# Two small SBUF tiles made larger in a two-layer hybrid decoder trunk

## The chip, the cores and the metric

The kernel runs on one NeuronCore of one Trainium2 chip, in one launch. The metric is the device time of one execution in microseconds (us); several executions are timed and their median is given. One further execution is recorded by the hardware profiler: its span runs from the first to the last instruction.

The engines are TensorE (PE; its weight loads are shown as PEld), VectorE (DVE), ScalarE (ACT), GpSimd (POOL) and SyncE (SP, which here only issues DMAs).

## The reference

The kernel computes a trunk of two layers over 256 positions of width 1,024, in float32. Each layer normalises its input, projects it through one matrix of 1,024 x 3,584, runs three branches, gates them, and projects back with a residual:

```python
def hybrid_layer(x, ...):
    hn = rms_norm(x, norm_gain)
    proj = jnp.einsum('bsd,de->bse', hn, w_in)
    a_q, a_k, a_v, a_g, b_x, b_g, c_q, c_k, c_v, c_g = jnp.split(proj, ...)
    y_a = dilated_attention(rope(a_q), rope(a_k), a_v) * silu(a_g)    # 8 heads of 64
    y_b = rg_lru_branch(b_x, conv_w, ...) * silu(b_g)                 # width 256
    y_c = stick_breaking_attention(c_q, c_k, c_v) * silu(c_g)         # 4 heads of 64
    y = jnp.concatenate([y_a, y_b, y_c], axis=-1)
    return x + jnp.einsum('bse,ed->bsd', y, w_out)
```

A last normalisation follows the second layer. The branch b begins with a causal convolution of width 4 along the sequence.

## The kernel before

**Arithmetic.** Each large product is made from three float32r products. A tile is split into a high part (rounded to float32r by ACT) and a low part (what is left, by DVE), and hi x hi, hi x lo and lo x hi are added in PSUM. The normalised input is the tile `xx`, which holds `xh` and `xl` side by side. Weights come from HBM in chunks of 128 x 2,048 through staging tiles `st` and are split into `whi` (line 109) and `wlo` (line 110). The gated branch outputs are split into `yh` and `yl` (lines 413 and 414), the rotated q and k into tiles that the profile calls `qk` (lines 498 and 499).

**Matmul lines.** Line 169 is the first projection, made while the first chunks arrive. Line 211 is the helper `mm3`, used by several projections: those whose moving tile is xx (256 columns, stationary tile whi or wlo; named `pp<-xx,whi`), those of a_v and c_v in layer 1 (stationary xx, moving whi or wlo), and the output projection (stationary yh or yl, moving whi or wlo, 512 columns). In the names of the profile the two operands of a matmul stand in no fixed order. Lines 330 and 327 make the paired projections of layer 1: line 330 takes xh and xl together as 512 moving columns, line 327 takes 256. Line 513 makes the scores of the dilated attention, four heads at a time on 32 rows each. Line 461 holds transposes.

**Order of the work.** PE's instructions run in the order in which the program writes them. SP issues the weight loads in the order of use, limited by free staging tiles. ACT and DVE split the weights ahead of PE into four buffers each for whi and wlo.

**Where tiles lie.** SBUF tiles come from the pools cst, wst, wsp, sb and wk, laid one behind the other in this order in each partition; inside a pool they lie in the order in which their tags first appear, with sizes rounded up to 32 bytes. So a size of one tile sets where everything behind it starts. The start of each tile in bytes, past a multiple of 512:

| pool | tiles in order | start before |
|---|---|---|
| cst | xres, con, then `tiny` | 256 |
| cst | ones, c8, nc8 | 288, 288, 320 |
| cst | rp, rp0, rb, gn (and gf) | 352 |
| wst, wsp | st (5 buffers), whi and wlo (4 each) | 352 |
| sb | xx, th, it, va, vc, gw_t, qc (q1), kc (k1), then `bxp` (and av) | 352 |
| sb | xc, xs, rt, bg, cg, q0, k0, yh, yl, the qk tiles | 384 |
| wk | scr (7 buffers), sw, wv | 448 |
| wk | pr, low | 64, 192 |

The slices that PE reads within xx, whi, wlo, yh, yl and the qk tiles step by multiples of 512 bytes, so they have their tile's start.

**The two tiles.** `tiny` holds one number per partition, a bias of 1e-19 for a logarithm in `lru_scan`. `bxp` holds the input of the convolution with three zeros ahead of each of its two halves:

```python
def conv(mid):
    dve.memset(bxp[:, :, 0:3], 0.0)
    proj_to(bxp[:, :, 3:259], CH_BX, mid)
    for b in range(2):
        ...
        for j in (2, 1, 0):
            dve.scalar_tensor_tensor(xc[:, b, :], bxp[:, b, j:j + 256], ...)
```

The tile av of `lru_scan` takes the same place as bxp later in the layer.

Of the kernel before, what the change touches and what calls it, by code (L numbers as in the profile page):

```python
# [9 lines left out]
F32 = mybir.dt.float32  # L10
# [5 lines left out]
P = 128  # L16
# [32 lines left out]
def trunk_kernel(ctx: ExitStack, tc: tile.TileContext, x, first_x, first, wpack, prm_d, gatew, gains, consts, rope, out):  # L49
# [3 lines left out]
    cst = ctx.enter_context(tc.tile_pool(name="cst", bufs=1))  # L53
    wst = ctx.enter_context(tc.tile_pool(name="wst", bufs=WST))
    wsp = ctx.enter_context(tc.tile_pool(name="wsp", bufs=4))
    sb = ctx.enter_context(tc.tile_pool(name="sb", bufs=1))
# [125 lines left out]
    diag = con[:, C_DG:C_DG + 255]  # L182
    nc.sync.dma_start(out=con, in_=consts)

    tiny = cst.tile([P, 1], F32, name="tiny")
    dve.memset(tiny, 1e-19)
    ones = cst.tile([P, P], F32, name="ones")
    dve.memset(ones, 1.0)
# [108 lines left out]
    for l in range(L):  # L297
# [245 lines left out]
            turned(prob, h0, range(3), to)  # L543
            return heads

        bxp = sb.tile([P, 2, 259], F32, name="bxp", tag="bxp")
        xc = sb.tile([P, 2, S], F32, name="xc", tag="xc")
        xs = sb.tile([P, 2, S], F32, name="xs", tag="xs")
        rt = sb.tile([P, 2, S], F32, name="rt", tag="rt")
# [248 lines left out]
```

## Time and profile before

| | before |
|---|---|
| median of 3 runs | 249.22 us (248.92 to 249.33) |
| profiled execution, span | 247.5 us |
| outside the span, against the median | 1.7 us |
| PE busy | 239.7 us, 97% |
| PE weight loads busy | 212.8 us, 86% |
| DVE busy | 193.4 us, 78% |
| ACT busy | 170.8 us, 69% |
| POOL busy | 11.6 us, 5% |
| share of PE in the chain that ended last | 85% |
| DMA | 43.90 MB, mean 177 GB/s |

The page gives no time of its own for the profiled execution beside its span, so the span is what sums are made against. A busy share is a mean over the whole span. The chain that ended last is followed back from the last instruction, at each step to what released it. A matmul's duration contains its latency, which overlaps with the next matmul; the pace at which matmuls follow each other is shorter than that duration.

### The profile page before, as it was taken

To read this page: it belongs to the slowest core of one execution; us is meant where nothing else is said; L and a number is where in the kernel's file an instruction comes from. 1 tells how busy PE (TensorE), PEld (TensorE's weight loads), DVE (VectorE), ACT (ScalarE), POOL (GpSimd) and SP (SyncE) were. 2 spreads that over 40 slices of the span, in tenths; PEclk is the share of its full clock that TensorE was granted. 3 is DMA by queue.
4 is the path that set the end of the run, shared out by engine and by line. 5 is a ranking of instruction groups with operands and counts; after the bars stand their busy time and mean duration, and the time that the engine had idled before them with its cause. 6 is when DMAs were issued, how large, how long until landed. Compare 5 with 4: busy or idle time off the path is not lost.

```text
span 247.5 us, 4741 instructions
## 1 busy us (share of the span) xinstructions
PE 239.7 (97%) x1753; PEld 212.8 (86%) x1753; DVE 193.4 (78%) x454; ACT 170.8 (69%) x368; POOL 11.6 (5%) x45
## 2 busy tenths in 40 slices
PE   8999999999999999999999999999999999999990
PEld 4889999998998899878889988888889889987870
DVE  4884798979999789985693666999999867984253
ACT  3779988844688499964662775876589749992142
POOL 0037000000100000000000000000000000000000
PEclk9999999999999999999999999999999999999997
DMA  6989987377737732267258387506461752000022
GB/s 209 399 284 411 355 318 277 117 234 242 222 98 212 256 98 74 89 218 272 103 171 252 106 304 269 173 3 216 145 193 68 238 209 85 3 0 0 3 85 85
DMA packets 13174, 43.90 MB, mean 177 GB/s; under 512 B 1632, under 2 KB 2144, under 8 KB 13152
## 3 DMA queue, kind: packets, MB, share of 16 engines
q1 hardware_dynamic: 12384, 42.30, 50.6%
q10 hardware_dynamic: 576, 0.79, 0.9%
q0 software_dynamic: 192, 0.52, 0.8%
q8 instruction: 14, 0.23, 0.3%
q14 instruction: 8, 0.07, 0.1%
HBM read 42.03 MB, written 1.05 MB: 174 GB/s over the span
## 4 chain that ended last, share of the span: by engine, by line
PE 85%; DVE 5%; DMA 4%; ACT 2%; SPq 0%; issue 0%; ACTq 0%; DVEq 0%
PE pp L211 44%; PE pp L330 11%; PE s L211 9%; PE pp L327 5%; PE s L169 3%; PE s L461 3%; DMA st<-first 3%; PE s L513 2%; PE y L425 2%; DMA st<-w_pack 2%; PE pp L169 2%; DVE sw L452 2%; DVE wlo L110 1%; PE pp L425 1%; PE s L441 1%; PE s L572 1%
## 5 line engine op out<-in xcount | busy, mean ns | idle before, releaser
L110 DVE TENSOR_TENSOR wlo<-st,whi 128x512 fp32r<-128x512 f32 x132 | 84.0, 684 | 12.4 <-ACT whi L109 12.0
L109 ACT ACTIVATE whi<-st 128x512 fp32r<-128x512 f32 x132 | 74.0, 628 | 20.5 <-PE pp L211 7.6
L211 PE MATMUL pp<-xx,whi 128*128 128x256 f32 x480 | 63.3, 285 | 0.0
L211 PEld LDWEIGHTS pp<-xx,whi 128*128 128x128 f32 x480 | 59.6, 192 | 0.8 <-issue 0.3
L211 PE MATMUL pp<-xx,wlo 128*128 128x256 f32 x240 | 33.7, 283 | 0.0
L211 PEld LDWEIGHTS pp<-xx,wlo 128*128 128x128 f32 x240 | 31.0, 192 | 0.0
L330 PE MATMUL pp<-xx,whi 128*128 128x512 f32 x112 | 29.3, 396 | 0.0
L330 PEld LDWEIGHTS pp<-xx,whi 128*128 128x128 f32 x112 | 20.1, 189 | 3.9 <-ACT scr L83 0.3
L83 ACT ACTIVATE pr<-scr,mn 128x128 f32<-128x128 f32 (+1 forms) x32 | 14.1, 441 | 8.7 <-DVE mn L520 8.7
L77 ACT ACT_TABLE_LOAD x13 | 16.7, 1283 | 1.9 <-PEq L791 1.7
L327 PEld LDWEIGHTS pp<-xx,wlo 128*128 128x128 f32 x112 | 15.3, 190 | 1.1
L327 PE MATMUL pp<-xx,wlo 128*128 128x256 f32 x112 | 15.6, 282 | 0.0
L211 PE MATMUL pp<-whi,yh 128*128 128x512 f32 x48 | 14.6, 405 | 0.0
L211 PE MATMUL pp<-whi,yl 128*128 128x512 f32 x48 | 14.1, 396 | 0.0
L211 PE MATMUL pp<-wlo,yh 128*128 128x512 f32 x48 | 14.1, 395 | 0.0
L211 PEld LDWEIGHTS pp<-whi,yl 128*128 128x128 f32 x48 | 9.0, 188 | 2.2
L211 PEld LDWEIGHTS pp<-wlo,yh 128*128 128x128 f32 x48 | 9.0, 188 | 2.2
L211 PEld LDWEIGHTS pp<-whi,yh 128*128 128x128 f32 x48 | 8.6, 188 | 2.1 <-issue 0.3
L413 ACT ACTIVATE yh<-scr 128x512 fp32r<-128x512 f32 x8 | 5.0, 631 | 7.5 <-DVE scr L411 7.4
L169 PE MATMUL s<-whi,xx 128*128 128x512 f32 (+1 forms) x36 | 9.9, 396 | 0.1
L520 DVE CUSTOM_DVE_ANT_0 scr<-s,con 128x128 f32<-128x128 f32 (+1 forms) x32 | 9.2, 352 | 0.0
L333 ACT ACTIVATE low<-pp 128x256 f32<-128x256 f32 x14 | 5.3, 377 | 5.2 <-PE pp L330 5.2
(175 smaller groups left out, 359.3 us busy)
## 6 DMA issues: line engine op xcount, KB each, us to landing
st<-w_pack SPq DMA_DIRECT2D x66, 512.0 KB, 5.1
st<-first SPq DMA_DIRECT2D x7, 512.0 KB, 6.1
xres<-x_in SPq DMA_DIRECT2D x2, 512.0 KB, 7.5
gw_t<-gate_w SPq DMA_DIRECT2D x2, 256.0 KB, 6.8
gn<-gains SPq DMA_DIRECT2D x1, 512.0 KB, 6.9
xs<-xc POOLq DMA_DIRECT2D x4, 128.0 KB, 4.8
gf<-gains SPq DMA_DIRECT2D x1, 512.0 KB, 6.3
out<-scr SPq DMA_DIRECT2D x2, 256.0 KB, 2.1
```

Source lines behind the costliest of these rows:

```text
L77: load = act.preload_act_table_set(name)
L83: i = dep(act.activation(*a, **k), loaded["load"])
L109: split[l, c] = act.activation(hi[:, ws], st[:, ss], AF.Copy)
L110: dve.tensor_sub(lo[:, ws], st[:, ss], hi[:, ws].bitcast(F32))
L169: pe.matmul(ps[t][:, c0 - base:c1 - base], a[:, k, t * P:(t + 1) * P], b[:, c0:c1], start=k == 0 and i == 0 and c0 == base, stop=k == NK - ...
L211: pe.matmul(ps, a(k), b(k), start=first and i == 0, stop=last and i == len(seq) - 1)
L327: pe.matmul(ps[:, 0:S], lo[:, k, cs], xh[:, k, :], start=False, stop=False, skip_group_check=True)
L330: pe.matmul(ps, hi[:, k, cs], xx[:, k].rearrange("p h t -> p (h t)"), start=i == 0, stop=i == len(seq) - 1, skip_group_check=True)
L333: act.activation(low, ps[:, S:2 * S], AF.Copy, scale=sc)
L425: pe.matmul(y[hr, p * 128 + o:p * 128 + 256], vt[:, s0, hs], wts[i][s0], start=s0 == 0, stop=s0 == 1)
L461: pe.transpose(tp[:, i * P:(i + 1) * P], tiles[h0 + h][:, j * P:(j + 1) * P], ident)
L520: dve.tensor_tensor_reduce(xs[:, cs], sps[h][:, cs], nmask[:, cs], -0.125, 3e38, ALU.add, ALU.min, mn[:, t:t + 1])
```

## The change

`tiny` is allocated with 48 columns in place of 1, and its first column is used as before. `bxp` is allocated with 320 columns for each half in place of 259, and the same 259 are used. Nothing else in the program is changed.

```diff
-    tiny = cst.tile([P, 1], F32, name="tiny")
+    tiny_t = cst.tile([P, 48], F32, name="tiny")
+    tiny = tiny_t[:, 0:1]
     dve.memset(tiny, 1e-19)
...
-        bxp = sb.tile([P, 2, 259], F32, name="bxp", tag="bxp")
+        bxp = sb.tile([P, 2, 320], F32, name="bxp", tag="bxp")
```

By the sizes, tiny takes 192 bytes of each partition in place of 32, and bxp 2,560 in place of 2,080. What lies behind tiny moves by 160 bytes, what lies behind bxp by 640. The starts past a multiple of 512 then are 0 for rp, rp0, rb, gn, st, whi, wlo and all tiles of sb. They stay at 256 for xres and con, and become 448 for ones, 64 for scr, sw and wv, 192 for pr and 320 for low.

## The prediction

> **What bounds the kernel now.** I read three stretches of the span first: the load at the start, the body, and the tail after the last matmul.
>
> ```profile
> core 0: us, PE busy (x) PEld busy (x) DVE busy (x) ACT busy (x) POOL busy (x), PEclk, DMA share, GB/s
> 0.00:9.60 9.60, 8.28 (x37) 5.67 (x37) 4.68 (x14) 4.27 (x7) 0.43 (x9) 1.00 0.80 279
> 9.60:241.20 231.60, 231.38 (x1716) 207.13 (x1716) 186.45 (x435) 164.86 (x356) 11.19 (x36) 1.00 0.52 176
> 241.20:247.50 6.30, 0.00 (x0) 0.00 (x0) 2.28 (x6) 1.67 (x5) 0.00 (x0) 0.78 0.22 83
> ```
>
> In the body PE is busy 231.38 of 231.60 us at a granted clock of 1.00. Nothing that DVE, ACT or the queues save there can show, unless they become the limit; what would show is a change in the pace at which matmuls follow each other. That pace I read from the chain of work that ended last (start, duration, engine and line, count).
>
> ```profile
> 2.10 6.20 DMA st<-first
> 60.13 14.58 PE pp L211 x120
> 74.72 1.32 PE s L461 x12
> 112.78 2.80 PE s L211 x12
> 124.85 5.45 PE s L211 x24
> 134.04 5.47 PE s L211 x24
> 144.00 0.95 PE pp L327 x8
> 144.95 1.84 PE pp L330 x8
> 232.73 8.41 PE pp L211 x36
> ```
>
> A float32r matmul of 256 columns comes every 14.58 us / 120 = 121.5 ns (0.95 / 8 = 119 at L327). One of 512 columns comes every 5.45 / 24 = 227 or 5.47 / 24 = 228 ns where the stationary tile is xx (the a_v projection of layer 1), every 1.84 / 8 = 230 ns at L330, but every 2.80 / 12 = 233 or 8.41 / 36 = 234 ns where the stationary tile is yh or yl (the output projection). The groups by line and shape say the same in other numbers (mean ns of one; they contain the matmul's latency, so only their differences count):
>
> ```profile
> L211 PE MATMUL pp<-xx,whi 128*128 128x256 f32 x480 | 63.3, 285 | 0.0
> L211 PE MATMUL pp<-xx,wlo 128*128 128x256 f32 x240 | 33.7, 283 | 0.0
> L330 PE MATMUL pp<-xx,whi 128*128 128x512 f32 x112 | 29.3, 396 | 0.0
> L327 PE MATMUL pp<-xx,wlo 128*128 128x256 f32 x112 | 15.6, 282 | 0.0
> L211 PE MATMUL pp<-whi,yl 128*128 128x512 f32 x48 | 14.1, 396 | 0.0
> L211 PE MATMUL pp<-wlo,yh 128*128 128x512 f32 x48 | 14.1, 395 | 0.0
> L211 PE MATMUL s<-whi,xx 128*128 128x512 f32 x32 | 8.3, 390 | 0.0
> L211 PE MATMUL s<-wlo,xx 128*128 128x512 f32 x16 | 4.3, 389 | 0.0
> L211 PE MATMUL s<-whi,yh 128*128 128x512 f32 x16 | 4.7, 395 | 0.0
> L211 PE MATMUL s<-wlo,yh 128*128 128x512 f32 x16 | 4.7, 395 | 0.0
> ```
>
> The last four rows matter most. Moving tile (whi or wlo), width and kind of PSUM tile (s) are the same; only the stationary tile differs, xx or yh, and the pair of 389 and 390 stands against 395. Among what differs is the place in SBUF: whi, wlo and xx all start at 352 bytes past a multiple of 512, yh and yl at 384. So an effect of addresses of about 6 ns per matmul may be in this trace already, and the change moves exactly these addresses.
>
> **The change part by part.** It adds and removes no instruction, wait or transfer. tiny takes 192 bytes in place of 32 and bxp 2,560 in place of 2,080, so cst behind tiny, st, whi, wlo, xx and the first part of sb move by 160 bytes, and what lies behind bxp by 640. Six costs follow.
>
> *The two tiles themselves: 0.* tiny is still written and read through one column. bxp keeps its widths; its second half begins at byte 1,280 in place of 1,036, and the convolution reads it at element offsets 0, 1 and 2.
>
> ```profile
> L561 DVE SCALAR_TENSOR_TENSOR xc<-bxp,prm_t,xc 128x256 f32<-128x256 f32 x12 | 5.4, 479 | 0.1
> L160 DVE SCALAR_TENSOR_TENSOR xx<-st,x,xx 128x256 fp32r<-128x256 f32 x7 | 3.4, 479 | 0.9 <-ACT xx L153 0.9
> ```
>
> Reads shifted by 4 bytes each cost 479 ns, like the same operation elsewhere.
>
> *DVE and ACT on moved tiles: 0.* The splits of weights (tiles at 352), of y (scr at 448, yh at 384) and of q and k (384) cost the same:
>
> ```profile
> L110 DVE TENSOR_TENSOR wlo<-st,whi 128x512 fp32r<-128x512 f32 x132 | 84.0, 684 | 12.4 <-ACT whi L109 12.0
> L414 DVE TENSOR_TENSOR yl<-scr,yh 128x512 fp32r<-128x512 f32 x8 | 5.5, 688 | 2.8 <-ACT yh L413 2.8
> L499 DVE TENSOR_TENSOR qk<-k,qk 128x512 fp32r<-128x512 f32 x4 | 2.7, 685 | 1.2 <-ACT qk L498 1.2
> L109 ACT ACTIVATE whi<-st 128x512 fp32r<-128x512 f32 x132 | 74.0, 628 | 20.5 <-PE pp L211 7.6 <-DMA st<-w_pack 7.6 <-PE s L211 4.9
> L413 ACT ACTIVATE yh<-scr 128x512 fp32r<-128x512 f32 x8 | 5.0, 631 | 7.5 <-DVE scr L411 7.4
> ```
>
> 684 against 688 and 685, 628 against 631. The bounds for 132 pairs are 132 x (685 - 684) = 0.1 us dearer and nothing cheaper, and it lies under PE in any case. If that cover went, 0.1 us is what it would cost.
>
> *DMA: 0 on the sum, 0.2 us either way at most.* Only the first 6.20 us of loading are on the path. A tile that starts at a multiple of 256 before (xres) lands no sooner than one at 352 (st, gf):
>
> ```profile
> st<-w_pack SPq DMA_DIRECT2D x66, 512.0 KB, 5.1
> xres<-x_in SPq DMA_DIRECT2D x2, 512.0 KB, 7.5
> gf<-gains SPq DMA_DIRECT2D x1, 512.0 KB, 6.3
> ```
>
> These medians contain queueing, so they only say that no gain stands out; as a bound I take 3% of 6.20 us, an estimate from the spread in pace between the quoted matmul rows (227 to 234) for want of a nearer one.
>
> *The weight loads: 0.* They are as long from yh at 384 as from xx at 352:
>
> ```profile
> L211 PEld LDWEIGHTS s<-whi,xx 128*128 128x128 f32 x32 | 5.9, 188 | 1.2
> L211 PEld LDWEIGHTS s<-whi,yh 128*128 128x128 f32 x16 | 2.9, 188 | 0.5
> ```
>
> *The output projection: -1.1 us.* There are 3 x 48 + 3 x 16 = 192 matmuls with yh or yl (three kinds on pp, three on s, of which the rows above show four). Before, stationary (384) and moving tile (352) are 32 bytes out of step; with xx they are in step (352 and 352). After the change all of them are at 0, so in step. If being in step is what gives 227.5 (the mean of 227.1 and 227.9) in place of 233.3, the term is 192 x 5.8 ns = 1.1 us. The bounds are 0 (the difference has another cause) and a rise elsewhere (third rival). All of it is on the path: PE is the limit in both stretches, 98 to 124 and 215 to 241 us. What is late next is the weights, and these are ahead:
>
> ```profile
> ACT whi L109 <- PE pp L211: 7.6, 4, 2.7
> ```
>
> ACT waits 7.6 us for PE to free a weight buffer, so the supply outlasts a PE that is 1.1 us faster.
>
> *The other float32r matmuls: 0.* Their two operands are in step before (352, 352) and after (0, 0). Whether 0 itself is better or worse than 352 no row of full-height matmuls shows. The nearest row is that of the dilated scores, where both operands lie at 384, a multiple of 128:
>
> ```profile
> L513 PE MATMUL s<-qk,qk x96: 272/277/360, 59.0 to 200.9; 32*128 32x256 f32 x96
> ```
>
> Its median is 277 ns against means of 283 and 285, which speaks for a gain of up to 6 ns, but these matmuls run four at a time on 32 rows each, so I carry it into a rival and not into the sum.
>
> Sum: 0 + 0 + 0 + 0 - 1.1 + 0 = -1.1 us. Against the profiled execution: 247.5 - 1.1 = 246.4 us of span. The 1.7 us between that span and the median of 249.22 lie outside the instructions and stay, which gives 248.1 us.
>
> One rule is weighed here. By the Trainium skill, page "TensorE: Matmul & The Clock Gate", section "Back-to-back issue gap", a warm matmul is followed by the next after N / 2.4 + 2.5 ns, which is 216 ns for 512 columns and 109 for 256. The trace disagrees (227 to 234 and 121.5), and no row says why. If poor alignment were the whole reason, 720 + 112 matmuls at 12 ns and 112 + 48 + 192 at about 14 ns would make an estimate of 15 us by that page; that goes beyond every row of this case and is not in the sum.
>
> **The rivals.**
>
> *First, nothing changes: 249.2 us.* The 6 ns of the output projection may come from the order of its terms or from its steps of 1,024 bytes against xx's 2,048, and PE's pace may not know addresses. For it: the equal weight loads, DVE and ACT rows above; L330, in step as well, has 396 like the rows with yh. Against it: L330 alternates with 256-column matmuls at L327, while the four s rows are like against like. The Trainium skill, page "SBUF — State Buffer", section "Specifications (TRN2)", speaks for this rival too: it gives cachelines of 16 bytes, and 352, 384 and 0 are all multiples of 16. No run here shows a line size.
>
> *Second, a good deal faster: 243.4 us.* A start at 352 may cost each matmul one more read step. With 64 bytes as the step (the smallest power of two that 352 misses; an assumption) that is 16 columns. A column costs (227.5 - 121.5) / 256 = 0.41 ns, so 6.6 ns, close to the 6 ns by which 277 undercuts 283. On 480 + 240 + 112 + 112 + 192 + 48 = 1,184 matmuls that makes 7.8 us. Not all of it can come through, since the splitting engines are full beside PE in layer 0:
>
> ```profile
> 60.50:74.00 13.50, 13.50 (x115) 13.50 (x114) 13.50 (x52) 9.49 (x26) 1.25 (x2) 1.00 0.56 173
> ```
>
> There DVE is busy 13.50 of 13.50 us. I take half to all, 3.9 to 7.8 us, with the middle 5.8. Against it: yh at 384 is a multiple of 128, and its matmuls are the slow ones.
>
> *Third, slower: 249.9 us.* A stationary tile at a multiple of 128 bytes may itself be what costs the 6 ns (yh at 384), and the change puts all of them there. It decides as soon as the s rows with xx go from 389 to 395: then 48 matmuls lose 6 ns and the 112 at L330 some 233.3 - 230 = 3.3 ns, together 0.66 us. If the 256-column ones follow, 832 x 6 ns = 5.0 us more, 254.9. Against the latter: the 277 ns at L513, with both tiles at a multiple of 128.
>
> **How the numbers follow.** In step is better, output projection alone: 0.35, 248.1 us, own range 247.6 to 248.6. Nothing changes: 0.25, at 249.2. Faster throughout: 0.20, around 243.4. Slower: 0.20, of which 0.15 near 249.9. A difference of 0.2%, 0.5 us, is about what a measurement of this kernel can tell from no change (the three runs span 248.92 to 249.33). The range of 243.5 to 250.5 leaves out the better half of the second rival (0.10) and the worse end of the third (0.05). Faster: 0.34 of the first case and most of the second, less its thin end, 0.53; within 0.2%: 0.27; slower: 0.20.
>
> **What the profile after would show.** If the main case holds, the s rows with yh fall from 395 to about 389, the chain's twelve at L211 from 2.80 to about 2.73 us, and 256-column matmuls stay at 283 to 285; DVE, ACT and weight loads keep 684, 628 and 188. Rows with xx at 395 are the third rival, 256-column rows near 277 the second. I am wrong in the mechanism if the time moves while all these rows stand still.

## The result, and the profile after

The changed kernel takes 247.71 us (median of 6 runs, 247.23 to 248.61) against 249.23 us (6 runs, 248.92 to 250.34) for the kernel before: a ratio of 0.9934, 95% interval 0.991 to 0.9958. Two later comparisons, told below, gave 0.9963 and 0.9976. One of the seven runs of the kernel at +192 below took 249.79 us at a lower granted clock, 0.988, and is counted in its median but not in its ratio. The profiled execution has a span of 246.5 us, 1.0 us less than before, and a time of its own of 248.61 us. In the new kernel.py every line behind 185 has a number higher by one, so line 211 is now 212, 327 is 328, 330 is 331.

The chain of work that ended last, in order of time (start, us, engine and line, count), kernel after:

```profile
60.13 14.58 PE pp L212 x120
98.60 2.76 PE s L212 x12
112.56 2.72 PE s L212 x12
115.28 6.80 PE pp L212 x30
124.33 5.44 PE s L212 x24
133.52 5.47 PE s L212 x24
144.43 1.84 PE pp L331 x8
215.26 2.76 PE s L212 x12
231.94 8.17 PE pp L212 x36
```

The same view of the kernel before, for the pieces that the prediction did not show:

```profile
98.64 2.79 PE s L211 x12
115.58 7.00 PE pp L211 x30
215.79 2.79 PE s L211 x12
```

The starts say where the microsecond went. The 120 matmuls of layer 0 begin at 60.13 us in both. The first output projection begins at 98.64 before and at 98.60 after, and the work behind it at 124.85 and at 124.33: 0.48 us gone. From there to the second output projection it is 90.94 us before and 90.93 after. The second begins at 215.79 and 215.26 and ends with its last 36 matmuls at 241.14 and 240.11: 0.50 us gone. So 0.98 of the 1.03 us lie in the two output projections, and 0.05 us elsewhere. Inside the output projections, twelve matmuls went from 2.80 to 2.72 us, thirty from 7.00 to 6.80, thirty-six from 8.41 to 8.17 (234 to 227 ns each). The 256-column matmuls (14.58 for 120), those with stationary xx (5.44 and 5.47 for 24) and line 331 (1.84 for 8) kept their pace. That both executions begin the 120 matmuls at 60.13 us is chance, as the next execution of the changed kernel shows.

The groups by line and shape of the kernel after (busy time, mean ns of one):

```profile
L212 PE MATMUL pp<-xx,whi 128*128 128x256 f32 x480 | 63.8, 285 | 0.0
L331 PE MATMUL pp<-xx,whi 128*128 128x512 f32 x112 | 29.2, 396 | 0.0
L212 PE MATMUL pp<-whi,yl 128*128 128x512 f32 x48 | 13.8, 389 | 0.0
L212 PE MATMUL s<-whi,xx 128*128 128x512 f32 x32 | 8.3, 390 | 0.0
L212 PE MATMUL s<-whi,yh 128*128 128x512 f32 x16 | 4.6, 392 | 0.0
L212 PEld LDWEIGHTS pp<-wlo,yh 128*128 128x128 f32 x48 | 9.0, 188 | 1.9
L110 DVE TENSOR_TENSOR wlo<-st,whi 128x512 fp32r<-128x512 f32 x132 | 84.0, 684 | 12.6 <-ACT whi L109 12.3
L109 ACT ACTIVATE whi<-st 128x512 fp32r<-128x512 f32 x132 | 73.8, 628 | 20.2 <-DMA st<-w_pack 7.5 <-PE pp L212 7.4 <-PE s L212 4.9
```

The rows with yh or yl fell from 395 and 396 to 389 to 392, onto the row with xx, which stayed at 390. One row stands apart, `pp<-whi,yh`; it fell from 405 to 400. DVE, ACT and the weight loads keep 684, 628 and 188 ns.

### The profile page after: what moved, and what is told of

Its sections match the earlier page's. It is cut to its first block, busy times and chain, and to the rows that moved or that the text cites. A ratio compares the mean times of both kernels' runs of the same rounds, so it can differ in the third digit from the quotient of the medians.

```text
span 246.5 us, 4741 instructions
## 1 busy us (share of the span) xinstructions
PE 238.6 (97%) x1753; PEld 212.4 (86%) x1753; DVE 193.3 (78%) x454; ACT 170.5 (69%) x368; POOL 11.3 (5%) x45
## 4 chain that ended last, share of the span: by engine, by line
PE 94%; DMA 2%; DVE 1%; ACT 1%; SPq 0%; issue 0%; ACTq 0%
PE pp L212 51%; PE pp L331 11%; PE s L212 9%; PE pp L328 5%; PE s L169 4%; PE s L462 3%; PE s L514 2%; PE y L426 2%; DMA st<-first 2%; PE pp L169 2%; PE s L442 1%; PE pp L426 1%; PE s L573 1%; PE s L260 1%; DVE xres L689 0%; ACT scr L243 0%
```

## The experiments

Three questions were open: whether the gain comes from being in step or from the multiple of 512; what "in step" is; and whether it is good for all matmuls. Offsets below are the start of xx, yh or yl less that of whi and wlo, whichever of the two is the stationary operand. In kernels with a gap tile (a tile that nothing reads, there to move what lies behind it) line 211 is numbered 213, 327 is 329, 330 is 332, and 109 and 110 are 110 and 111.

**The changed kernel again.**

> The changed kernel again, timed on the same chip as the others. Theory A (stationary and moving tile in step, meaning the same start modulo some power of two): s rows with yh at 389 to 392 ns, as many as with xx, and 1.0 us less than before from 192 matmuls of the output projection. The rest of the 1.5 us by which the median fell is either scatter between runs (then nearer 1.0 here) or something at the loads (then 1.5 again).

Measured: 248.20 us (12 runs) against 248.83 (29 runs), ratio 0.9963, interval 0.9943 to 0.9983. The chain again has 14.58 us for 120, 2.72 for 12 and 8.17 for 36, the same to a hundredth of a us, but it comes to the 120 matmuls about 1 us sooner than the first execution of the same program, which had 60.13:

```profile
59.15 14.58 PE pp L212 x120
```

So executions of one program scatter by about 1 us ahead of this point. The first comparison's 1.5 us is taken for the 1.0 us of the paces and scatter; the two intervals overlap.

**One tile at a time.** First bxp alone, so that whi, wlo, xx, yh and yl all start at 352 past a multiple of 512:

```diff
-        bxp = sb.tile([P, 2, 259], F32, name="bxp", tag="bxp")
+        bxp = sb.tile([P, 2, 320], F32, name="bxp", tag="bxp")
```

> Only bxp is made larger, tiny stays. Starts past a multiple of 512: st, whi, wlo, xx 352, and yh, yl, qk now 352 too (384 before). So everything PE reads is in step, and nothing is at a multiple of 512. Theory A: rows with yh fall from 395 to 389 or 390, and the whole gain of the changed kernel (about 1.0 us) is here. Theory B (multiples of 64 or 512 bytes are what is fast): rows with yh stay at 395 or rise, no gain. If loads into st at a multiple of 512 give a part of the gain, this kernel is about 0.5 us slower than the changed one.

Then tiny alone, so that whi, wlo and xx start at 0 and yh and yl at 32:

```diff
-    tiny = cst.tile([P, 1], F32, name="tiny")
+    tiny = cst.tile([P, 48], F32, name="tiny")[:, 0:1]
```

> Only tiny is made larger, bxp stays. Starts: st, whi, wlo, xx 0, and yh, yl, qk 32. Weights and xx are at multiples of 512, the output projection is out of step by 32 bytes as before. Theory A: rows with yh stay at 395, time as before (249.2), less 0.5 us if the loads into st count. Theory B: 256-column rows and rows with xx improve, rows with yh improve by the moving tile at least.

The groups by line and shape, bxp alone and then tiny alone:

```profile
L211 PE MATMUL pp<-whi,yl 128*128 128x512 f32 x48 | 13.8, 389 | 0.0
L211 PE MATMUL s<-wlo,yh 128*128 128x512 f32 x16 | 4.6, 390 | 0.0
```

```profile
L211 PE MATMUL pp<-whi,yl 128*128 128x512 f32 x48 | 14.1, 395 | 0.0
L211 PE MATMUL s<-wlo,yh 128*128 128x512 f32 x16 | 4.7, 395 | 0.0
```

With bxp alone: 248.28 us, ratio 0.9961 (0.9942 to 0.9981), the same as the whole change on that chip. With tiny alone: 248.65 us, ratio 0.9984 (0.9964 to 1.0005), and the rows with yh and yl are where they were before. So the multiple of 512 has no part in the gain that these runs could see. What counts is that bxp's size brings yh and yl to the same place as whi and wlo.

**xx out of step instead.** A tile that nothing reads is put ahead of the pool sb, with bxp sized so that yh and yl stay in step (the write of the tile is one short POOL instruction at the start):

```diff
+    pad = ctx.enter_context(tc.tile_pool(name="pad", bufs=1))
     sb = ctx.enter_context(tc.tile_pool(name="sb", bufs=1))
...
+    gps.memset(pad.tile([P, 8], F32, name="gap"), 0.0)
...
-        bxp = sb.tile([P, 2, 259], F32, name="bxp", tag="bxp")
+        bxp = sb.tile([P, 2, 316], F32, name="bxp", tag="bxp")
```

> A tile of 32 bytes is put ahead of xx and bxp is 316 columns wide, so xx starts at 384, whi, wlo, st at 352, yh and yl at 352. Now the output projection is in step and all products with xx are out of step by 32 bytes. One small GpSimd memset is added, off the path. Theory A: rows with yh at 389 or 390 (gain of 1.0 us), s rows with xx go from 389 to 395 (48 matmuls, 0.3 us lost), and the 256-column rows (283, 832 of them) show for the first time what being out of step costs there: between 0 and 6 ns each, so 0 to 5 us lost; in all 248.5 to 253.5 us. Theory B: no row changes by more than 1 ns.

The chain and then the groups of the kernel with xx at +32:

```profile
83.19 14.20 PE pp L213 x120
123.15 5.60 PE s L213 x24
```

```profile
L213 PE MATMUL pp<-xx,whi 128*128 128x256 f32 x480 | 61.8, 281 | 0.0
L213 PE MATMUL s<-whi,xx 128*128 128x512 f32 x32 | 8.4, 396 | 0.0
```

Measured: 247.09 us (6 runs), ratio 0.9914 (0.9882 to 0.9946). For 512 columns with stationary xx the theory held: 5.60 / 24 = 233 ns, and 396 where the kernel in step has 390. For 256 columns it failed with the opposite sign: 14.20 / 120 = 118.3 ns in place of 121.5, and 281 in place of 285. The time therefore fell below the 248.5 to 253.5 us that were expected. Line 332, 512 columns with moving xx, went from 1.84 to 1.87 us for 8. Against +32, being in step is the better state at 512 columns and the worse one at 256.

**Which offset.** Four kernels with the gap tile at other sizes, each timed and profiled in one execution:

```diff
+    gps.memset(pad.tile([P, 16], F32, name="gap"), 0.0)    # +64; 32 columns: +128; 64 columns: +256
...
+        bxp = sb.tile([P, 2, 320], F32, name="bxp", tag="bxp")
```

At +64, +128 and +256 yh and yl move with xx. For -32 the gap has 120 columns and bxp its old size, which leaves yh and yl in step.

> xx, yh, yl, qk start 64 bytes (mod 512) past the start of whi and wlo (416 against 352). A tile of 64 bytes ahead of xx makes the shift, one GpSimd memset is added. If what counts is the offset within 64-byte blocks, all rows look in step: rows with yh and s rows with xx at 389 to 390 ns, 256-column rows at 283 to 285, pace 120. If it is the offset within 128, 256 or 512 bytes, they look out of step as at 32 bytes: yh and s rows with xx at 395, 256-column pace below 120.

> The same with 128 bytes (480 against 352). In step if the block is 64 or 128 bytes, out of step if it is 256 or 512.

> The same with 256 bytes (96 against 352). In step if the block is 64, 128 or 256 bytes, out of step if it is 512.

> xx starts 32 bytes before the phase of whi and wlo (320 against 352), yh and yl in step with them (352). If the block is 64 bytes, -32 is the same as +32: 256-column pace near 118.6 ns, s rows with xx at 395, yh at 389 to 390, as in the kernel with xx 32 bytes ahead. If the sign counts, the 256-column pace is 120 or above.

The chain at +64, +128, +256 and -32, in this order (120 matmuls of 256 columns with moving xx; 24 of 512 with stationary xx; 36 of 512 with yh or yl):

```profile
82.51 14.34 PE pp L213 x120
123.13 5.60 PE s L213 x24
230.47 8.41 PE pp L213 x36
```

```profile
84.54 14.45 PE pp L213 x120
125.15 5.61 PE s L213 x24
233.23 8.38 PE pp L213 x36
```

```profile
83.56 14.58 PE pp L213 x120
123.89 5.47 PE s L213 x24
231.53 8.17 PE pp L213 x36
```

```profile
85.80 14.39 PE pp L213 x120
125.91 5.60 PE s L213 x24
233.55 8.17 PE pp L213 x36
```

At +256 every row is that of the kernel in step, at the other three xx is out of step. So what counts is the offset inside a block of 256 bytes. At -32 the piece shown is the second 120 of layer 0; the first took 15.92 us in a stretch where the granted clock was 0.89, which also raises a mean over that run. The single times (247.66, 250.28, 248.36 and 250.47 us beside 249.38) are not read as verdicts: one execution each, where the 29 runs of the kernel before told above spread from 248.29 to 250.43.

The Trainium skill, page "SBUF — State Buffer", section "Specifications (TRN2)", gives cachelines of 16 bytes. By lines of that size alone, offsets of 32, 64 and 128, all multiples of 16, would be alike and equal to 0; the runs have 5.60 and 5.61 us against 5.47. What sits behind a period of 256 bytes no run here shows.

**A version that uses both signs.** xx out of step by +64 and by +192 (that is, -64), yh and yl in step, and the changed kernel beside them on the same chip:

```diff
+    gps.memset(pad.tile([P, 16], F32, name="gap"), 0.0)    # +64; 48 columns for +192
...
+        bxp = sb.tile([P, 2, 280], F32, name="bxp", tag="bxp")    # +64; 264 for +192
```

> whi and wlo stay at 352 past a multiple of 512; xx lies 64 bytes further on (416), yh, yl and the qk tiles at 96, in step with whi and wlo counted modulo 256. My theory after the first eight runs (the offset of xx against whi and wlo inside a block of 256 bytes sets the pace, with opposite signs for 512 and 256 columns) expects: 512 columns with yh or yl at 228 ns (s rows 390 to 392), 512 columns with stationary xx at 233 ns (s rows 395), 256 columns with moving xx about 119 ns (rows 281 and 279), line 327 at 116 ns. Against the kernel before that is 192 x -5.2 ns = -1.0 us, 48 x +5.8 ns = +0.3 us, 720 x -2.4 ns = -1.7 us and 112 x -2.4 ns = -0.3 us: -2.7 us in all, of which up to about 1 us may be lost where layer 0 waits for the splits of weights: 246.1 to 247.1 us beside a before of 248.8, a ratio of 0.989 to 0.993. The rival, that the gain of the run with xx at +32 was chance of that one chip and only the output projection counts, expects the ratio of the changed kernel, 0.993 to 0.996.

> Like the run with xx at +64, with xx 192 bytes past whi and wlo inside a block of 256 (start 32, against 352), and yh, yl and the qk tiles in step. If only the distance to the nearest place in step counts, +192 is 64 bytes short of 256 and equals +64: 256 columns at 119 ns, ratio 0.989 to 0.993. If the sign counts, as the run at -32 suggests (mean 122.2 there, with some matmuls at 116), 256 columns stay at 121.5 to 122 and 512 columns with stationary xx at 233 ns: -1.0 + 0.3 = -0.7 us, ratio 0.997.

> The changed kernel once more, beside the two with xx out of step on the same chip: 256 columns with moving xx at 122 ns, 512 columns at 228 ns everywhere. My theory expects a ratio of 0.993 to 0.997 against before, above that of the run with xx at +64 by 0.003 to 0.006; the rival expects the two to be equal.

Measured against 249.06 us (18 runs): +64 has 247.42 us, ratio 0.9939 (0.9916 to 0.9962); +192 has 247.10 us (7 runs), ratio 0.9913 (0.988 to 0.9945); the changed kernel has 248.45 us, ratio 0.9976 (0.9958 to 0.9994). The intervals of +192 and of the changed kernel don't meet; those of +64 and of the changed kernel just do, so for +64 the rival that expects them equal is not excluded by its time. The chain of +64 and then of +192:

```profile
84.33 14.33 PE pp L213 x120
124.40 5.60 PE s L213 x24
```

```profile
82.46 13.81 PE pp L213 x120
122.28 5.50 PE s L213 x24
198.22 14.33 PE pp L213 x120
```

At +64 the paces came as expected, 14.33 / 120 = 119.4 ns; the time, 247.42 us, lies above the expected 246.1 to 247.1. At +192 both expectations failed by the paces, though the ratio lies in the range of the first. 13.81 / 120 = 115.1 ns is the best piece of 120 so far, and 5.50 / 24 = 229 ns came where 233 was expected. So for 512 columns with stationary xx neither the distance to the nearest place in step (+64 has 5.60) nor the sign alone sets the pace.

For 256 columns the offset does not settle the pace alone. In layer 1 of the execution at +192 the same 120 take 14.33 us, as at +64. Groups of 24 show two paces at both offsets. Here are the first kernel at +64, the second one at +64, and +192, where the first row of each is the same group of matmuls in the program:

```profile
74.64 2.72 PE pp L213 x24
```

```profile
76.36 2.83 PE pp L213 x24
```

```profile
74.58 2.73 PE pp L213 x24
190.24 2.83 PE pp L213 x24
```

That is 113 or 118 ns each, where the kernel before has 2.87 us, 120 ns. So a group at +64 or at +192 runs at one of two paces, and 119.4 against 115.1 ns is not shown to be a difference between the two offsets. What chooses the pace is open.

**The same offset from another start.** whi and wlo at a multiple of 512 as in the changed kernel, xx 192 bytes further on, yh and yl in step:

```diff
-    tiny = cst.tile([P, 1], F32, name="tiny")
+    tiny = cst.tile([P, 48], F32, name="tiny")[:, 0:1]
...
+    gps.memset(pad.tile([P, 48], F32, name="gap"), 0.0)
...
+        bxp = sb.tile([P, 2, 264], F32, name="bxp", tag="bxp")
```

> The changed kernel's start for whi and wlo (a multiple of 512) together with the offset of the run before (xx 192 bytes further on, yh, yl and the qk tiles at 256, in step modulo 256). If only the offset inside a block of 256 counts, the paces repeat: 256 columns with moving xx at 117 ns, 512 columns with yh or yl at 228 ns, with stationary xx at 229 ns, line 330 at 233 ns, line 327 at 115 ns, and a ratio of 0.988 to 0.9945 against before. If instead the place of xx itself counts (32 past a multiple of 256 in the run before, 192 here), 256 columns go back to some 119 to 121.5 ns and the ratio to 0.994 to 0.998.

The chain, with pieces of the stretch of layer 0 that leads to its second group of 120:

```profile
61.90 2.41 DVE wlo L111 x4
75.39 1.66 ACT whi L110 x3
82.77 13.81 PE pp L213 x120
122.63 5.50 PE s L213 x24
142.72 1.86 PE pp L332 x8
190.80 2.74 PE pp L213 x24
198.68 13.81 PE pp L213 x120
229.15 8.17 PE pp L213 x36
```

Measured: 245.87 us (6 runs) against 249.28 (11 runs), ratio 0.9869 (0.9825 to 0.9914), the lowest time of all kernels here. The ratio is a little below the expected range, which its interval reaches into. The paces repeat from another start, 13.81 us now in both layers, so it is the offset of xx against whi and wlo that allows the better pace, not the place of xx. Which of the two paces a group takes still varies: the 24 at 190.80 took 2.74 us here and 2.83 at 190.24 in the run before.

If all 720 matmuls ran at the better pace, 121.5 - 115.1 = 6.4 ns would be worth 4.6 us beside the 1.0 us of the output projection, less 0.3 us at line 332 (112 / 8 x 0.02 us, 1.86 against 1.84); between the medians 3.4 us came. Two reasons are seen, and their shares were not measured. Some groups run at the slower pace: the 32 matmuls with whi from 183.6 us have a median duration of 281 ns, the 80 with whi from 198.6 us 276. And in this execution the chain runs from 55 to 77 us not over PE but over DVE (7.8 of some 20 us are splits of weights, the rest the convolution, a softmax and the rotations) and then ACT; PE waits for it. The two groups of 120 in layer 0 begin 23.7 us apart (at 58.96 and 82.70 in the timeline), against 23.9 before (60.13 and 84.05). In the run at +192 before it the chain stayed on PE there, and they begin 23.0 us apart (59.44 and 82.46). So this hand-over is seen in one of two executions.

## Why the prediction was right

It was right in the mechanism and nearly in the size; by its own steps:

- **The output projection, -1.1 us.** Right: the stretches lost 0.48 + 0.50 = 0.98 us, and the twelve went to 2.72 us where 2.73 was foretold. The size was 12% too large, because the two pieces from which the 5.8 ns were read do not stand for all: those pieces fell by 6.7 ns per matmul, the groups of 24 by 4.6 (5.59 to 5.48 us) and the first twelve by 2.5; the whole, 0.98 us / 192, is 5.1 ns. That the stationary tile's place against the moving tile is the cause was a guess from one pair of rows, 389 against 395. bxp alone and tiny alone then showed it. That being in step is better is no general rule: against every other offset tried it is the slower state at 256 columns. The forecast took no harm because the change left those matmuls in step.
- **The two tiles, DVE, ACT, DMA, weight loads, other matmuls: 0.** Held. The rows of DVE, ACT, weight loads and 256 columns stand where they stood, and the two projections are 90.94 and 90.93 us apart.
- **Only the first load on the path.** This reading was wrong. The chain of the kernel before leaves PE at 38.31 us for DVE and ACT, and then holds a second load:

```profile
52.31 4.73 DMA st<-w_pack
```

  It did not touch the sum: in the kernel after the chain stays on PE there, and the gain came behind it.

- **Next late: the weights.** Held for 1 us, since the changed kernel kept its gain. With 256 columns faster as well, PE waited in one execution for DVE, which the prediction had seen full in this stretch (13.50 of 13.50 us), and for ACT; in the other it did not.
- **From span to median.** The span came to 246.5 us, forecast 246.4. But the 1.7 us taken for what lies outside it was mis-sized: the profiled execution after has 248.61 - 246.5 = 2.1 us, and the 58 later runs of the kernel before have 2.06 to 2.24. With as much, the profiled execution before took about 249.6 us (an estimate) and was one above its median, and the forecast would have been 248.5 us. The median moved by more (1.5 us) in the first comparison and by less (0.6 us) in the second and third; 0.98 us of 249.2 is a ratio of 0.9961, just outside the first interval and inside the other two.
- **First rival, nothing changes.** Refuted: the matmuls with yh and yl follow their place against whi and wlo in every run.
- **Second rival, a read step less from a multiple of 64 or more.** Refuted: with xx, whi and wlo at 0 the 256-column row stays at 285.
- **Third rival, slow at a multiple of 128.** Refuted: the s rows with xx at 0 stay at 390.
- **The estimate of 15 us that was left out** rested on the Trainium skill, page "TensorE: Matmul & The Clock Gate", section "Back-to-back issue gap": 109 ns for 256 columns and 216 for 512. The section gives them for a matmul on its own, and 131 ns at 512 columns for a stream of weight loads and matmuls, which is what runs here. The best offset came to 115.1 and 227 ns; none reached the page's figures for these float32r matmuls, each with its own weight load. The best offset takes back 6 of the 12 ns at 256 columns; at 512 none was faster than being in step.

## What to carry to other kernels

Where PE is the bound, compare the pace of matmuls that differ only in the tile they read: two rows of one shape with different means are a lead to where their operands lie. What can then be tuned is the start of the stationary tile against the moving tile, inside a block of 256 bytes, by the size of any tile ahead of them; the best value depends on the width, so try several and read the pace from the chain, not the time from one run. And look first at who feeds PE: in one of two executions at +192 a faster PE waited in layer 0 for DVE and ACT.

## What the runs showed of the hardware that was not expected

- The pace of a float32r matmul depends on the offset of its two SBUF operands inside 256 bytes, not on where either lies: 0 and 256 are alike, and +192 gave 115.1 ns from 352 and from 0.
- At +64 and +192 one offset has two paces at 256 columns, 113 or 118 ns by groups of 24, and a group can change from one to the other between executions (2.83 and 2.74 us).
- At 256 columns being in step is the slowest of the offsets tried; by pieces of 120, 121.5 ns at 0, 118.3 at 32, 119.5 at 64, 120.4 at 128, 115.1 or 119.4 at 192 (that is, -64), 119.9 at 224 (-32).
- At 512 columns with stationary xx it is the fastest: 227 to 228 ns at 0, 229 at 192, 233 to 234 at 32, 64, 128 and 224. With moving xx (line 330) 8 take 1.84 us at 0, 1.83 at 64 and 1.86 to 1.87 at the others.
